# Moving a hybrid decoder layer's residual to DRAM for two thirds of its MLP, and computing four more quads by seven products

## The chip, the cores and the metric

The kernel runs on one core of a Trainium2 chip. The metric is the device time of one execution in microseconds; lower is better. An execution's own time is a little longer than its span, which runs from the first to the last instruction of the program.

## What is computed

One decoder layer on a sequence of 256 tokens, all in float32: an RMS norm, a combined input projection, eight attention heads and a pooling mixer, an output projection into the residual `x`, and then the part that this change is about, a gated MLP with a causal depthwise convolution between the up-projection and the gate:

```python
D_MODEL, SEQ, D_FF, CONV_WIDTH = 2048, 256, 5632, 3

def conv_ffn(h, w_up, conv_w, conv_b, w_down):
    u = h @ w_up
    u_pad = jnp.pad(u, ((0, 0), (CONV_WIDTH - 1, 0), (0, 0)))
    y = conv_b
    for i in range(CONV_WIDTH):
        y = y + conv_w[i] * u_pad[:, i:i + S]
    gate, val = jnp.split(y, 2, axis=-1)
    return (jax.nn.silu(gate) * val) @ w_down
...
    x = x + jnp.concatenate([a, m], axis=-1) @ w_out[l]
    x = x + conv_ffn(rms_norm(x, ffn_norm_g[l]), w_up[l], conv_w[l], conv_b[l], w_down[l])
```

## The kernel before

**Precision.** Every float32 matrix product is made of three float32r products: high by high, low by high and high by low, where `high` is the operand rounded to float32r and `low` what the rounding left. ACT makes the high part (`split_high`, L215), DVE the low part (`split_low`, L223 and L229).

**Chunks and steps.** All weights lie in DRAM as chunks of 128 x 2048 floats (1 MB). The program is a list of steps, two to a chunk. SP loads the chunks in order into four buffers, `raw`; the load of a chunk is issued when DVE has split the chunk that lay in its buffer (`release`, L290 and after). The high parts have a ring of four chunks, the low parts one of three, and splits are written five to six steps ahead of the products that use them. `hooks` (`after(u, f)`) hang further work on a step, in program order; each engine runs its own instructions in that order.

**The MLP** goes in thirds of 8, 8 and 6 hidden blocks of 256 features (`THIRDS`). The up stage of a third has 64 steps (48 in the last), each of 16 products into `ps_feat` (L313, L315); ACT and DVE evacuate, scale and add the convolution's taps, apply the gate, and split the result into `hid`. The down stage then multiplies `hid` by `w_down` in two passes of 1024 output columns (`down_pair`, `bp` 0 and 1). A pass goes quad by quad, a quad being one chunk: 2 blocks of hidden features by 2 halves of tokens by 2 halves of columns. An ordinary quad (`quad`, L982) takes 8 block products, 24 matmuls of 512 columns. A mixed quad (`quad_sums`, L919) takes 7 block products of sums and differences (Strassen's scheme in Winograd's form), 21 matmuls. The table `MIXED` names the mixed quads of each pass: 6 and 5 in a long third, 4 and 4 in the last, 30 in all.

**Sets.** A mixed quad needs sums of its weight blocks, in high and low parts: a set tile of 128 x 3072 (1.5 MB), of which there are four (`SETS`: 0 in the tag `s0`, 1 in the temporaries, 2 and 3 in the places `h2` and `h1` of `x2h`, the MLP's input, whose last blocks are therefore stored in DRAM as `tail` and loaded again before the next third). It also needs sums of its token halves, made by POOL (`token_sums`, L893) and kept in 20 cells, `sx`. Some sets are made in place in the down stage (`seven_sums`, DVE on `raw`). The other 16 (`STORED`: third, step, pass and quad they are for, steps ahead) are made during the up stage: SP loads the weights once more into `w` (1 MB, L251), ACT and DVE make the sums (L270 to L275, L243 to L247), POOL stores the differences `t` (512 KB, L262) and the set `s` (512 KB and 1 MB, L264). In the down stage SP loads the set back (1.5 MB, `load_set`, L267) and the quad's `raw` takes half of its data from `t`.

**Ends of a pass.** The residual sum `x2` (128 x 2 x 2048 floats, 2 MB) stays in SBUF. At the end of a pass the seven products' parts are added to it by DVE (`add_part`, L1035 to L1043); the ordinary products' banks are copied by ACT to a staging tile `st` in the place `s0` (`close`, L1089) and added to `x2` by two accumulating DMAs of 512 KB on POOL's queue (`add_by_dma`, L1012). Set 0 can be written again when these have landed. After the second pass of a long third (`behind`) the parts are copied to `st` first, and the additions follow in the next third's first steps.

## Time and profile before

| | |
|---|---|
| median of 3 runs | 1003.54 us (1003.36 to 1003.68) |
| the profiled execution | 1003.49 us, span 1001.6 us |
| PE busy | 997.1 us (100% of the span) |
| DVE busy | 858.9 us (86%) |
| ACT busy | 662.0 us (66%) |
| POOL busy | 144.3 us (14%) |
| DMA | 290.44 MB, 290 GB/s over the span |
| first long third, up stage and down stage | 179.7 and 79.6 us |
| second long third | 177.5 and 79.6 us |
| last third | 133.1 and 60.5 us |

A busy time is the time in which an engine had an instruction under way; the stages are read from the chain of waits, by the first matmul of each. The DMA share that the profile gives for a stretch is the mean busy share of the core's 16 DMA engines, which the queues of SP and POOL use together; it can come out slightly over 1. "To landing" is the time from a DMA's issue to the semaphore that tells its arrival.

### The profile page before, as it was taken

Reading aid. Unit: us, or ns where it says so; the run is one execution under the profiler, and the core shown is the slowest. Engines: PE = TensorE matmul, PEld = TensorE weight load, DVE = VectorE, ACT = ScalarE, POOL = GpSimd, SP = SyncE. Lnnn points to the kernel's source line nnn. Section 1 sums busy time; section 2 is a strip of 40 time slices with the busy share of each in tenths; the row PEclk is TensorE's granted clock in tenths of the full one; section 3 lists DMA queues with packets and bytes.
Section 4 is the critical chain, followed back from the end, with each engine's and each line's share of the span. In section 5 each row is a group of like instructions: output and inputs, shape, how many; then the busy total and the mean of one; then the engine's idle time right before and its main releaser. Section 6 shows DMA issues by size and latency. Waiting matters only on the chain.

```text
span 1001.6 us, 13775 instructions
## 1 busy us (share of the span) xinstructions
PE 997.1 (100%) x5205; PEld 856.7 (86%) x5205; DVE 858.9 (86%) x946; ACT 662.0 (66%) x1000; POOL 144.3 (14%) x178
## 2 busy tenths in 40 slices
PE   9999999999999999999999999999999999999998
PEld 8888888888888888888888888888888888888887
DVE  6989677898987989897987799998789869898898
ACT  6945575555566877787556577777766567777652
POOL 0220004700000122120000021321000002121110
PEclk9999999999999999999999999999999999999999
DMA  9775554474468899999898988989889897899894
GB/s 343 290 240 204 172 186 168 169 285 142 172 241 304 328 345 317 340 333 358 316 369 345 303 282 326 350 318 339 324 313 366 323 337 276 319 336 335 344 296 145
DMA packets 47170, 290.44 MB, mean 290 GB/s; under 512 B 5416, under 2 KB 6312, under 8 KB 19456
## 3 DMA queue, kind: packets, MB, share of 16 engines
q1 hardware_dynamic: 37456, 247.22, 67.4%
q0 software_dynamic: 9648, 42.34, 12.8%
q8 instruction: 41, 0.67, 0.3%
q14 instruction: 25, 0.20, 0.1%
HBM read 244.06 MB, written 39.19 MB: 283 GB/s over the span
## 4 chain that ended last, share of the span: by engine, by line
PE 99%; DVE 0%; issue 0%
PE ps_feat L313 35%; PE ps_feat L315 18%; PE ps_down L982 12%; PE ps_p L919 10%; PE ps_tok L300 9%; PE ps_down L919 7%; PE ps_v L307 4%; PE ps_pool L322 1%; PE ps_s L549 1%; PE ps_start L390 0%; PE ps_down L1004 0%; PE ps_T L536 0%; PE ps_x2T L766 0%; PE ps_av L582 0%; PE ps_eT L571 0%; PE ps_av L583 0%
## 5 line engine op out<-in xcount | busy, mean ns | idle before, releaser
L313 PE MATMUL ps_feat<-x2h,wh 128*128 128x512 f32 x1408 | 488.8, 392 | 0.0
L315 PE MATMUL ps_feat<-x2h,wl 128*128 128x256 f32 x1408 | 393.6, 280 | 0.0
L215 ACT ACTIVATE wh<-raw 128x1024 fp32r<-128x1024 f32 x358 | 360.1, 1048 | 16.2 <-DMA raw<-in_wts 12.9
L313 PEld LDWEIGHTS ps_feat<-x2h,wh 128*128 128x128 f32 x1408 | 264.2, 188 | 58.2
L229 DVE TENSOR_TENSOR wl<-raw,wh 128x2048 fp32r<-128x2048 f32 x116 | 266.8, 2307 | 31.1 <-ACT wh L215 16.8
L315 PEld LDWEIGHTS ps_feat<-x2h,wl 128*128 128x128 f32 x1408 | 264.3, 188 | 0.1
L223 DVE TENSOR_TENSOR wl<-raw,wh 128x1024 fp32r<-128x1024 f32 x126 | 156.9, 1268 | 10.4 <-ACT wh L215 6.6
L270 ACT ACTIVATE s<-raw 128x512 fp32r<-128x512 f32 (+1 forms) x38 | 32.0, 841 | 77.9 <-DVE raw L247 66.2
L835 ACT ACTIVATE y<-fs,pv 128x256 f32<-128x256 f32 x88 | 52.2, 593 | 45.0 <-DVE fs L822 45.0
L893 POOL TENSOR_TENSOR s<-y 128x128 f32<-128x128 f32 x34 | 34.5, 1014 | 291.4 <-DVE y L870 150.4
L270 ACT ACTIVATE s<-w 128x512 fp32r<-128x512 f32 (+1 forms) x32 | 26.8, 839 | 31.7 <-DMA w<-in_wts 31.7
L1012 POOL DMA_DIRECT2D x<-st x13 | 11.6, 930 | 241.9 <-ACT st L1089 195.0
L313 PE MATMUL ps_feat<-xh,wh 128*128 128x512 f32 x128 | 46.3, 402 | 0.0
L275 DVE TENSOR_TENSOR s<-w,s 128x512 fp32r<-128x512 f32 (+1 forms) x32 | 31.1, 973 | 15.5 <-ACT s L270 15.4
L601 ACT ACTIVATE fs<-ps_feat 128x512 f32<-128x512 f32 (+1 forms) x46 | 26.0, 565 | 25.3 <-PE ps_feat L315 25.3
L836 ACT ACTIVATE tap<-fs,pv 128x256 f32<-128x256 f32 x84 | 41.6, 495 | 0.0
L838 ACT ACTIVATE fs<-fs,pv 128x256 f32<-128x256 f32 x88 | 39.4, 495 | 0.0
L605 DVE TENSOR_TENSOR fs<-ps_feat,fs 128x512 f32<-128x512 f32 (+1 forms) x46 | 30.2, 659 | 8.4 <-ACT fs L601 8.4
L264 POOL DMA_DIRECT2D s<-s x32 | 17.3, 542 | 132.8 <-DVE s L275 132.5
L315 PE MATMUL ps_feat<-xh,wl 128*128 128x256 f32 x128 | 35.8, 280 | 0.0
L982 PE MATMUL ps_down<-wh,hid 128*128 128x512 f32 x144 | 35.6, 389 | 0.0
L300 PE MATMUL ps_tok<-wh,xh 128*128 128x512 f32 x128 | 35.5, 399 | 0.0
(268 smaller groups left out, 1589.1 us busy)
## 6 DMA issues: line engine op xcount, KB each, us to landing
raw<-in_wts SPq DMA_DIRECT2D x161, 1024.0 KB, 6.5
s<-s SPq DMA_DIRECT2D x16, 1536.0 KB, 8.7
w<-in_wts SPq DMA_DIRECT2D x16, 1024.0 KB, 8.1
s<-s POOLq DMA_DIRECT2D x16, 1024.0 KB, 10.6
raw<-in_wts SPq DMA_DIRECT2D x20, 512.0 KB, 5.8
t<-t POOLq DMA_DIRECT2D x16, 512.0 KB, 5.7
s<-s POOLq DMA_DIRECT2D x16, 512.0 KB, 6.7
raw<-t SPq DMA_DIRECT2D x16, 512.0 KB, 6.6
```

The source lines that it names most:

```text
L215: nc.scalar.activation(wparts[u][0], raw_of(u), AF.Copy)
L223: nc.vector.tensor_tensor(wpart(u, "wl"), raw_of(u), wparts[u][0].bitcast(F32), op=OP.subtract)
L229: nc.vector.tensor_tensor(whole(c, "wl"), raws[c], whole(c, "wh").bitcast(F32), op=OP.subtract)
L270: nc.scalar.activation(parts[0], w, AF.Copy)
L300: nc.tensor.matmul(ps[:, t, :], act[:, k0 + k, a, t * P:(t + 1) * P], w[:, k * 512:(k + 1) * 512], start=(first and k == 0 and n == 0), st ...
L307: nc.tensor.matmul(ps[:, t, :], act[:, k, a, t * P:(t + 1) * P], w[i], start=(first and n == 0), stop=(last and n == 2))
L313: nc.tensor.matmul(ps, wh[:, ws], act[:, k, :, :], start=(first and n == 0), stop=False, skip_group_check=True)
L315: nc.tensor.matmul(ps[:, S:], wl[:, ws], act[:, k, 0, :], start=False, stop=(last and n == len(ks) - 1), skip_group_check=True)
L835: nc.scalar.activation(y[:, m, :], u[:, m, :], AF.Identity, scale=cw[m][2], bias=col(C_CB + f0_ + m))
L836: nc.scalar.activation(a[:, m, :], u[:, m, :], AF.Copy, scale=cw[m][1])
L919: nc.tensor.matmul(ps, act[a], w[i], start=(first and n == 0), stop=(last and n == 2), skip_group_check=skip)
L982: nc.tensor.matmul(bank(t, b), hid(j, h, t)[a], part(w, b if h == 0 else 1 - b)[i], start=(n == 0 and h == 0 and (fresh or j == normal and ...
```

## The change

Four more quads become mixed: `MIXED` now has 7 quads in the first and 6 in the second pass of each long third, 34 in all, and eight sets of each long third are stored instead of six, 20 in all. To make room, `x2` leaves SBUF: it is written to DRAM (`parked`, 2 MB in two DMAs on POOL's queue) just before and at the first step of the MLP, and its place takes a fifth set tile (set 4) and four more cells for token sums (`more`). It is loaded back at step 43 of the last third. In between, each pass of the long thirds makes its whole sum in `st` (ACT's copy of the banks becomes two additions by DVE in the first pass) and adds it by accumulating DMA to `parked` in DRAM. All stored sets are made in set 4's tile; the weights for those of the long thirds are loaded by turns into two places (`cl` and `s0`, the column `odd`), every 6 steps instead of every 8 for most; the differences are made in place. Only one of the two tail blocks of `x2h` is stored and loaded in a long third, since set 3 is not used there. The loads of stored sets move from SP's queue to POOL's.

```diff
-MIXED = {8: ((0, 2, 3, 4, 5, 6), (0, 2, 3, 5, 6)), 6: ((0, 2, 3, 4), (0, 1, 2, 3))}
-SETS = {8: ({2: 2, 4: 3, 5: 1, 6: 2}, {0: 3, 2: 2, 3: 1, 5: 0, 6: 1}), 6: ({2: 3, 4: 2}, {0: 1, 1: 3, 2: 0, 3: 1})}
-STORED = ((0, 10, 0, 0, 0, 8), (0, 18, 0, 0, 2, 4), (0, 26, 0, 0, 4, 7), (0, 34, 0, 0, 6, 6), (0, 42, 0, 1, 0, 6), (0, 50, 0, 1, 2, 6), (1, 10, 1, 0, 0, 8), (1, 18, 1, 0, 2, 4), (1, 26, 1, 0, 4, 7), (1, 34, 1, 0, 6, 6), (1, 42, 1, 1, 0, 6), (1, 50, 1, 1, 2, 6), (2, 10, 2, 0, 0, 8), (2, 18, 2, 0, 2, 4), (2, 26, 2, 0, 4, 7), (2, 34, 2, 1, 1, 8))
+MIXED = {8: ((0, 1, 2, 3, 4, 5, 6), (0, 2, 3, 4, 5, 6)), 6: ((0, 2, 3, 4), (0, 1, 2, 3))}
+SETS = {8: ({0: 0, 1: 4, 2: 2, 3: 0, 4: 4, 5: 1, 6: 2}, {0: 4, 2: 1, 3: 2, 4: 4, 5: 0, 6: 1}), 6: ({2: 3, 4: 2}, {0: 1, 1: 3, 2: 0, 3: 1})}
+STORED = ((0, 8, 0, 0, 0, 7, 0), (0, 14, 0, 0, 1, 6, 1), (0, 20, 0, 0, 2, 4, 0), (0, 26, 0, 0, 4, 4, 1), (0, 32, 0, 0, 6, 6, 0), (0, 38, 0, 1, 0, 6, 1), (0, 44, 0, 1, 3, 8, 0), (0, 50, 0, 1, 5, 5, 1), (1, 2, 1, 0, 0, 7, 0), (1, 10, 1, 0, 1, 6, 0), (1, 18, 1, 0, 2, 4, 0), (1, 24, 1, 0, 4, 4, 1), (1, 30, 1, 0, 6, 6, 0), (1, 36, 1, 1, 0, 6, 1), (1, 42, 1, 1, 3, 8, 0), (1, 50, 1, 1, 5, 5, 1), (2, 10, 2, 0, 0, 8, 0), (2, 18, 2, 0, 2, 4, 0), (2, 26, 2, 0, 4, 7, 0), (2, 34, 2, 1, 1, 8, 0))
...
-    def early_load(c):
-        w = late["early"] = keep.tile([P, CH], F32, name="w", tag="cl")
+    def early_load(c, odd):
+        late["early", c] = w = (late["pool"] if odd else keep).tile([P, CH], F32, name="w", tag="s0" if odd else "cl")
         nc.sync.dma_start(w, wts[c])
...
     def load_set(c, i):
-        nc.sync.dma_start(late["tile"][i].bitcast(F32), stored[c][1])
+        nc.gpsimd.dma_start(late["tile"][i].bitcast(F32), stored[c][1])
...
+    def park(b):
+        if b == 0:
+            late["parked"] = dram.tile([P, NT, D], F32, name="parked")
+        c = slice(1024 * b, 1024 * b + 1024)
+        nc.gpsimd.dma_start(late["parked"][:, :, c], late["x2"][:, :, c])
+
+    def parked():
+        t = late["pool"].tile([P, 1024 * MORE // 4 + 3072], F32R, name="more", tag="x2")
+        late["more"] = t[:, :256 * MORE].rearrange("p (n a t) -> p n a t", a=2, t=P)
+        s = late["tile"][4] = t[:, 256 * MORE:]
+        late["s"][4] = set_parts(s)
+
+    def back():
+        late["x2"] = late["pool"].tile([P, NT, D], F32, name="x2", tag="x2")
+        nc.sync.dma_start(late["x2"], late["parked"])
...
+        def add_parked(t, src):
+            add_by_dma(late["parked"][:, t, 1024 * bp:1024 * (bp + 1)], src)
+
+        def parts():
+            pa_, p5, p7 = box["aux"], box["p5"], box["p7"]
+            nc.scalar.activation(block(0), pa_[:, 0, :], AF.Copy)
+            nc.vector.tensor_tensor(block(1), pa_[:, 1, :], block(0), op=OP.add)
+            nc.vector.tensor_tensor(block(2), p7, block(1), op=OP.add)
+            nc.vector.tensor_tensor(block(3), p5, block(2), op=OP.add)
+            nc.vector.tensor_tensor(block(1), p5, block(1), op=OP.add)
...
         def close(u):
...
+            if kind == "down" and not final:
+                if behind:
+                    for t in range(NT):
+                        nc.scalar.activation(box["st"][:, 1024 * (t + 1):1024 * (t + 2)],
+                                             box["tok"][t].rearrange("p b n -> p (b n)"), AF.Copy)
+                else:
+                    for t in range(NT):
+                        x = box["st"][:, 1024 * t:1024 * (t + 1)]
+                        nc.vector.tensor_tensor(x, box["tok"][t].rearrange("p b n -> p (b n)"), x, op=OP.add)
+                        add_parked(t, x)
+                    new_set()
+                return
...
+    after(f0 - 3, lambda: park(0))
+    after(f0, lambda: park(1))
+    after(f0 + 4, parked)
...
+    after(third[-1][0] + 43, back)
...
-        after(third[n][0] + at - 4, lambda c=(u0 + 8 * nq + b * 2 * nq + 2 * j) // 2: early_load(c))
+        after(third[n][0] + at - 3, lambda c=(u0 + 8 * nq + b * 2 * nq + 2 * j) // 2, odd=odd: early_load(c, odd))
+        if odd:
+            after(third[n][0] + at + 6, new_set)
```

**How it moves instructions.** Two places are shown. The first is SP's queue at the start of the first long third's up stage: `raw` are chunk loads, `w` the extra loads for stored sets, `tail` the blocks of `x2h`. Before:

```order
L176 DMA raw<-in_wts 128x2048 x19
L794 DMA tail<-x2h 128x3072 x2
L251 DMA w<-in_wts 128x2048
L176 DMA raw<-in_wts 128x2048 x4
L251 DMA w<-in_wts 128x2048
```

And with the change:

```order
L178 DMA raw<-in_wts 128x2048 x18
L253 DMA w<-in_wts 128x2048
L178 DMA raw<-in_wts 128x2048
L813 DMA tail<-x2h 128x3072
L178 DMA raw<-in_wts 128x2048 x2
L253 DMA w<-in_wts 128x2048
L178 DMA raw<-in_wts 128x2048 x3
L253 DMA w<-in_wts 128x2048
```

Half of the tail is left, the first `w` stands ahead of it, and a `w` follows every three chunk loads where it followed every four.

The second place is POOL's queue in the first long third's down stage: `s`, `more<-s` are sets, `x<-st` and `parked<-st` the accumulating DMAs of a pass's end, with the semaphores that each waits for. Before, the loads of sets were not in this queue:

```order
L264 DMA s_3742<-s_1786 128x2048 [waits DMASW2_49,DVE_49]
L1012 DMA x_1783<-st 128x1024 [waits DMASW3_49,DMAHW4_49,DVE_49,Activation_49]
L1012 DMA x_1783<-st 128x1024 [waits DMASW4_49,Activation_49]
L1012 DMA x_1783<-st 128x1024 [waits DMASW5_49,Activation_49]
L1012 DMA x_1783<-st 128x1024 [waits DMASW6_49,Activation_49]
```

And with the change:

```order
L268 DMA more<-s_2831 128x3072 [waits DMASW4_49,DMASW6_49,DMASW2_49,DMASW7_49,DMASW1_49,PE_49]
L268 DMA s_4087<-s_2993 128x3072 [waits DMAHW1_49,DMASW5_49,PE_49]
L268 DMA more<-s_3145 128x3072 [waits DMASW4_49,PE_49]
L268 DMA s_4087<-s_3301 128x3072 [waits DMASW5_49,PE_49]
L268 DMA more<-s_3456 128x3072 [waits DMASW6_49,PE_49]
L268 DMA s_4087<-s_3618 128x3072 [waits DMASW7_49,PE_49]
L1032 DMA parked<-st 128x1024 [waits DVE_49,Activation_49]
L1032 DMA parked<-st 128x1024 [waits DMASW3_49,DVE_49]
L268 DMA s_4339<-s_3770 128x3072 [waits DMASW3_49,DMASW2_49]
```

The last row is set 0 of the second pass's sixth quad (`j` 5): it is loaded behind the two accumulations of the first pass and waits until both have landed, since they read `st`, which lies in the same place.

## Rows read from the trace of the kernel before

**Rows 1.** Page, the chain that ended last, by engine.

```profile
PE 99%; DVE 0%; issue 0%
```

**Rows 2.** Windows by stage: PE, PEld, DVE, ACT, POOL busy, clock, DMA share, GB/s.

```profile
288.40:468.10 179.70, 179.70 (x1044) 158.43 (x1043) 157.36 (x163) 136.42 (x224) 30.94 (x42) 1.00 0.88 320
468.10:547.70 79.60, 79.60 (x353) 65.89 (x352) 67.69 (x57) 47.42 (x58) 1.80 (x2) 1.00 0.92 346
547.70:725.20 177.50, 177.50 (x1026) 156.29 (x1025) 155.58 (x148) 130.44 (x205) 33.67 (x44) 1.00 0.90 322
725.20:804.80 79.60, 79.60 (x353) 65.92 (x352) 67.67 (x57) 47.44 (x58) 1.81 (x2) 1.00 0.90 338
```

**Rows 3.** Chain in order of time: start us, us, engine, tile, line, count.

```profile
468.12 2.75 PE ps_p L919 x12
...
472.91 5.44 PE ps_down L982 x24
478.35 2.72 PE ps_p L919 x12
481.07 2.04 PE ps_down L919 x9
...
507.59 2.72 PE ps_p L919 x12
...
981.48 1.22 DVE wl L223
```

**Rows 4.** Groups by form, DVE's part of a stored set: busy us, mean ns, idle before.

```profile
L243 DVE TENSOR_TENSOR t<-w 128x1024 f32<-128x1024 f32 x16 | 22.7, 1418 | 0.0
L275 DVE TENSOR_TENSOR s<-w,s 128x1024 fp32r<-128x1024 f32 x16 | 19.5, 1219 | 0.0
L275 DVE TENSOR_TENSOR s<-w,s 128x512 fp32r<-128x512 f32 x16 | 11.6, 726 | 15.5 <-ACT s L270 15.4
L247 DVE TENSOR_TENSOR w<-w 128x512 f32<-128x512 f32 x16 | 11.1, 692 | 0.6
L246 DVE TENSOR_TENSOR w<-w,t 128x512 f32<-128x512 f32 x16 | 10.9, 684 | 0.0
```

**Rows 5.** Windows of 22 us, up stage, a stored set in each.

```profile
354.00:376.00 22.00, 22.00 (x129) 19.35 (x128) 18.96 (x19) 17.12 (x28) 3.70 (x8) 1.00 0.97 348
376.00:398.00 22.00, 22.00 (x129) 19.39 (x128) 21.62 (x23) 16.59 (x27) 6.33 (x6) 1.00 0.90 319
```

**Rows 6.** Waits: engine, line, waited for: us in total, times, longest.

```profile
ACT s L270 <- DMA w<-in_wts: 31.7, 14, 4.1
...
DVE wl L229 <- PE ps_feat L315: 7.8, 8, 1.3
```

**Rows 7.** Page, DMA issues: queue, count, KB each, median us to landing.

```profile
s<-s SPq DMA_DIRECT2D x16, 1536.0 KB, 8.7
...
s<-s POOLq DMA_DIRECT2D x16, 1024.0 KB, 10.6
```

**Rows 8.** Line L267, loads of sets: SP's wait for one, and time to landing.

```profile
L267 SPq EVENT_SEMAPHORE  x20: 17/28/4635, 452.7 to 957.0; - x20
...
DMA to landing us min/median/max: 6.4/8.7/14.8
```

**Rows 9.** Timeline of ACT at the end of a first pass: start us, us, [idle before].

```profile
507.18 1.94 ACT L1089 ACTIVATE st<-ps_down 128x1024 f32<-128x1024 f32 x2 [2.41 <-PE ps_down L982]
...
524.68 0.63 ACT L270 ACTIVATE s<-raw 128x512 fp32r<-128x512 f32 x1 [0.57 <-DMA x<-st]
```

**Rows 10.** Windows of 20 us in the down stage.

```profile
488.00:508.00 20.00, 20.00 (x90) 16.57 (x89) 17.41 (x15) 11.62 (x13) 0.00 (x0) 1.00 0.99 380
508.00:528.00 20.00, 20.00 (x90) 16.57 (x89) 17.06 (x14) 10.07 (x12) 1.80 (x2) 1.00 1.02 356
```

**Rows 11.** Groups: DVE's addition of 1024 columns from PSUM.

```profile
L1037 DVE TENSOR_TENSOR x<-ps_p,x 128x1024 f32<-128x1024 f32 x6 | 7.3, 1222 | 0.1
```

More of the change, by code (lines that the diff above doesn't have):

```diff
@@ L83, in cells @@
         for kind, n in wants:
-            tag = next(t for t, (a, b) in free.items() if a + n <= b)
+            tag = next(t for t in (free if kind == "hid" else ("sx", "x2", "cl", "c"))
+                       if free[t][0] + n <= free[t][1] and (t != "cl" or g >= 6))
             out[-1].append((kind, tag, free[tag][0], n))
@@ L1093, in close @@
                     nc.gpsimd.dma_start(out[:, t, 1024 * bp:1024 * (bp + 1)], x2[:, t, :])
-            elif not mixer and not behind:
-                new_set()
         end = final and bp == 1
@@ L1115, in down_pair @@
                     acts.append(save_parts)
-                for i, n in enumerate(() if behind else range(2) if heads else (4, 0, 1) if apart else (4, 0, 1, 2, 3) if mixer else range(5)):
+                if kind == "down" and not final and not behind:
+                    if at == s_end + 1:
+                        acts += [new_st, parts]
+                        run.adds = True
+                for i, n in enumerate(() if kind == "down" and not final else range(2) if heads else (4, 0, 1) if apart else (4, 0, 1, 2, 3) if mixer else range(5)):
                     if at == s_end + 1 + (i * (rest - 1) // 5 if end else 0):
```

120 lines of the change are left out of this document (68 added, 52 removed).

## The prediction

> **What bounds the kernel now.** I read the chain of waits first, then the windows by stage, then the waits and the DMA rows of the long thirds. The chain is PE for 99% of the span, with no idle time to speak of [rows 1], at a granted clock of 1.00 in every stage [rows 2]: only fewer matmuls make the kernel shorter, and anything else shows only where PE is made to wait. The chain in order of time prices a quad: an ordinary one is 5.44 us for 24 matmuls, a mixed one 2.72 + 2.04 = 4.76 us for 21 [rows 3], both 0.227 us a matmul. One other piece of the chain is not PE, DVE's 1.22 us at 981.48 in the last third [rows 3], which the change does not touch.
>
> The reader is to see how near the helpers are to PE. In the up stages DVE is busy 157.36 of 179.70 and 155.58 of 177.50 us, and the DMA engines have a share of 0.88 and 0.90; in the down stages the share is 0.92 and 0.90 [rows 2]. DVE is nonetheless ahead: 8 times a split waited for PE to free its buffer [rows 6]. ACT waited 31.7 us in all for the extra weights `w` [rows 6].
>
> **The change, part by part.**
>
> *Matmuls.* Four ordinary quads become mixed: the order of PE has 96 fewer matmuls at the ordinary line and 84 more at the mixed one, so the change does what it says. 12 x 0.227 = 4 x (5.44 - 4.76) = **2.72 us less**, all on the path.
>
> *Two more stored sets in each long third, spaced closer.* DVE's part of one set is 1.42 + 1.22 + 0.73 + 0.69 + 0.68 = 4.74 us [rows 4]. Two windows of 22 us hold 18.96 + 21.62 = 40.58 us of DVE with two sets in them [rows 5]; without the sets that is 31.1 us in 44 us. A step of the up stage lasts about 177.5/64 = 2.77 us, so the rest of DVE's work is 1.96 us a step. At a set every 8 steps DVE has 15.7 + 4.7 = 20.4 of 22.2 us; at one every 6 it has 11.8 + 4.7 = 16.5 of 16.6 us. That is full, but not over, and there are only seven such intervals in the first long third and four in the second, with looser steps behind them. Over the second up stage it is 155.6 + 2 x 4.7 = 165 of 177.5 us. I price it at nothing, covered by DVE's lead of up to three chunks, of which a set uses 4.7 us and the following steps give it back. If the cover goes, what is late next is the low part of a chunk, and PE waits.
>
> *The extra weights* are issued at the same place between chunk loads as before (the order of SP), but no longer wait for the one `w` buffer to be free. That can only shorten ACT's 31.7 us [rows 6]. I book no gain, since PE did not wait for it.
>
> *Bytes.* A stored set costs 1 MB of `w`, 0.5 MB of `t` and 1.5 MB of `s` in the up stage (3.15 million bytes), and 1.57 million to load in the down stage. The second up stage moved 322 GB/s x 177.5 us = 57.2 MB [rows 2]; with two more sets 63.5 MB, or 358 GB/s. The down stages moved 27.5 and 26.9 MB; with two more loads less one tail load each they move 29.1 and 28.5 MB in 78.2 us, 372 and 364 GB/s. The first up stage also gains the parking (2.1 MB) and saves a tail store (1.6 MB): 64.3 MB in 179.7 us, 358 GB/s. Can the engines do it? At full share the rows of before carry 322/0.90 = 358 and 320/0.88 = 364 GB/s with stores among the loads, and 346/0.92 = 376 without; single windows reach 380 [rows 2, 10]. So the demand is just within reach, and I price it at nothing, with a rival below. The Trainium skill, page "DMA: Bandwidth & Descriptors", section "Where 436 GB/s comes from", says that a core's HBM-to-SBUF transfers are bound at about 358 GB/s. The trace speaks against a ceiling there: 380 GB/s over 20 us [rows 10]. By the page the down stages of the change would last 81.3 and 79.6 us, 4.5 us more in all than by my sum, as an estimate from the page 1005.7.
>
> *Set loads on POOL's queue.* SP no longer stops for them; one such stop took 4.6 us [rows 8], with chunk loads queued behind it. In return a set load shares each engine with the chunk loads. No row shows such a load on POOL's queue. The nearest are the same loads on SP, 6.4 / 8.7 / 14.8 us to landing [rows 8], and POOL's 1 MB stores, 10.6 us [rows 7]. Three places have little room.
> - Set 2 for the third quad (`j` 2) can't start before the up stage's last matmul, since it lies in `h2`. It is used after two mixed quads and half of a 2.72 us piece: 2 x 4.76 + 1.36 = 10.9 us. Set 4 for `j` 4 has the same 10.9 us after `j` 1. With 8.7 us both fit; bounds 0 and 14.8 - 10.9 = 3.9 us each.
> - Set 0 for `j` 5 of the second pass is behind the two accumulations, which read `st` in its place. Before, the second pass began at 507.59 [rows 3], and ACT was let go by the landed accumulations at 524.68 [rows 9]: 17.1 us later. In the change the set is used after 4.76 + 5.44 + 3 x 4.76 + 1.36 = 25.8 us. That leaves 8.7 us for the load, just its median. Against it stands that DVE now makes the sums (2 x 1.22 us, [rows 11]) where ACT copied (1.94 us, [rows 9]), 0.5 us later. For it stands that one tail load and one set load fewer run in SP's queue beside the accumulations, where the share was 1.02 [rows 10]. Bounds 0 and about 6.5 us each; I take 0.2 us in each long third, near the median row: **0.4 us more**.
>
> *Parking and return.* The two stores of 1 MB fall at the start of the first long third and the load of 2 MB at step 43 of the last, both beside chunk loads; no one reads `x2` for long after. Nothing; up to 1 us each if chunks come late. Accumulating into DRAM instead of SBUF is not in the trace; it takes the same two DMAs of 512 KB, and if it were slower, it would show in set 0's bound.
>
> *Ends of the passes.* DVE's five additions (some 5 us) become four of 512 columns and two of 1024, 4 x 0.69 + 2 x 1.22 = 5.2 us [rows 4, 11]; ACT loses two copies. PE needs the banks only after 2.72 us of the next pass. Nothing.
>
> **Sum.** 1003.49 - 2.72 + 0.4 = 1001.2 us for the profiled execution, which lies 0.05 us below the median of 1003.54. I forecast **1001.2 us**, 0.23% less.
>
> **The rivals.**
> 1. *Set loads come late, and the gain is eaten.* If each of the two set-0 loads is 1.5 us late and the four others 0.3 us, the change costs 4.2 us of waits: 1003.49 - 2.72 + 4.2 = 1005.0; anywhere from 1001.6 to 1005.5 it is within 0.2% of before. For it: the room equals the median, and half of such loads were slower. Against it: the slow ones in before stood in SP's queue behind chunk loads and each other.
> 2. *The DMA engines become the bound in the up stages, and the kernel is slower.* The place is the seven intervals of 6 steps in the first long third: 3 chunks, one `w` and 2.1 MB of stores are 6.3 MB in 16.6 us, 378 GB/s, against 358 to 364 at full share [rows 2]. At 360 an interval would last 17.5 us, 0.9 us more; ACT waits for `w` and for the set's tile to be stored, DVE for ACT. Over seven and four intervals that is 10 us of lateness, against a lead of DVE of some 4 us in each long third once a set's own 4.7 us are taken; so 10 - 8 = 2 us at least, and 6 us where the lead is less. With rival 1's waits: 1001.2 + 2 + 3 = 1006, up to 1010. It decides for slower when the up stages together lose over 4.5 us. Against it: no `w` is loaded after step 47, so the rest of the stage can make up for it, and a window with 348 GB/s at 0.97 passed with PE busy throughout [rows 5]. A ceiling at the page's 358 would be this rival in the down stages; with 380 measured [rows 10] I give it 0.02 of the 0.20.
> 3. *No wait at all*, and DVE's piece of 1.22 us [rows 3] goes too, as the sums are no longer made in the temporaries: 1003.49 - 2.72 - 1.2 = 999.6.
>
> **How the numbers follow.** A measurement of this kernel can tell some 0.2%, 2.0 us, from no change. My forecast, with waits under 0.7 us in all, has a chance of 0.43 and counts as faster; rival 1 has 0.33 and counts as the same; rival 2 has 0.20 and counts as slower; rival 3 has 0.04, faster. So faster 0.47, same 0.33, slower 0.20. The range goes from 999.9, just above rival 3, to 1006.5, which leaves out the upper half of rival 2 and the set loads' upper bounds (2 x 6.5 us); the faster cases alone lie in 999.6 to 1001.5.
>
> **What would show it.** Right: the chain is PE alone in both long thirds, their down stages at 78.2 us each and up stages at 179.7 and 177.5. Rival 1: pieces of the chain that are DMA `s<-s` or `more<-s`, at the sixth quad of a second pass or the third or fifth of a first; the accumulations' time to landing, and that of the set loads on POOL's queue, tell which. Rival 2: up stages longer, DMA share at 1 from step 8 on, ACT's waits for `w` or for `more` longer than 31.7 us in all, and DVE's splits on the chain. My forecast is wrong in its size if the ordinary line loses other than 96 matmuls or a mixed quad is not 4.76 us, and wrong in its reason if PE's time is as forecast but idle time appears in the last third.

## The result: slower by 0.64%, lost in DVE's lead and at the passes' ends

The changed kernel takes 1010.56 us in the median of 5 runs (1007.05 to 1011.19), the one before 1003.54 us (1003.07 to 1003.93): a ratio of 1.0064, with a 95% interval of 1.0046 to 1.0082. The forecast was 1001.2 us. The change also scatters over 4 us where the kernel before, run beside it, scatters over 0.9 (2.2 to 3.9 in the 9 to 23 runs of it beside the experiments). The profiled execution took 1009.67 us, with a span of 1007.6 us.

The chain of waits by engine, which was PE for 99% before [rows 1]:

```profile
PE 62%; DVE 20%; DMA 10%; issue 5%; ACT 3%; POOL 0%; DVEq 0%; SPq 0%; ACTq 0%; POOLq 0%
```

The long thirds' stages in the windows view, as in [rows 2] (stretch, its length, PE, PEld, DVE, ACT and POOL busy with their instructions, granted clock, DMA share, GB/s):

```profile
289.06:468.84 179.78, 179.78 (x1045) 158.51 (x1044) 167.77 (x175) 140.06 (x229) 45.37 (x55) 1.00 0.93 353
468.84:550.27 81.43, 79.43 (x347) 64.38 (x346) 67.59 (x59) 44.93 (x56) 5.09 (x8) 1.00 0.95 357
550.27:728.39 178.12, 177.77 (x1025) 156.28 (x1024) 162.10 (x157) 131.93 (x207) 43.37 (x56) 1.00 0.93 350
728.39:810.09 81.70, 79.39 (x347) 64.45 (x346) 69.40 (x61) 46.72 (x60) 5.08 (x8) 1.00 0.95 363
```

The clock is 1.00 throughout, so the loss is waiting. By the sum the down stages should last 79.59 - 1.36 = 78.23 us; they last 81.43 and 81.70 us, 6.7 us over plan together. The up stages are 0 and 0.6 us over. DVE's time in the up stages grew from 157.4 and 155.6 to 167.8 and 162.1 us. Inside the first one it hardly rests:

```profile
332.00:354.00 22.00, 22.00 (x129) 19.35 (x128) 21.62 (x22) 16.07 (x27) 7.11 (x8) 1.00 0.90 336
...
376.00:398.00 22.00, 22.00 (x128) 19.36 (x128) 21.58 (x23) 17.21 (x27) 5.08 (x6) 1.00 1.01 388
398.00:420.00 22.00, 22.00 (x129) 19.38 (x128) 21.62 (x22) 16.69 (x28) 6.00 (x7) 1.00 0.97 370
420.00:442.00 22.00, 22.00 (x129) 19.39 (x128) 21.58 (x23) 18.03 (x28) 6.89 (x10) 1.00 0.95 366
```

Before, such full windows took turns with looser ones (18.96 and 21.62 [rows 5]), 118.5 us of work in the 132 us from 310 to 442; now three full ones follow one another, and the same stretch holds 125.9. PE still runs without a gap here: it lives on splits made ahead. What that costs is seen in the chain in order of time (start, length, what), from the end of the up stage (468.84) to the start of the second pass:

```profile
451.88 2.20 DVE wl L231
454.08 0.61 DVE fs L606
454.79 0.55 issue
455.33 2.30 DVE wl L231
457.64 14.41 DMA raw<-in_wts
472.08 1.06 ACT wh L217
...
482.60 1.23 DVE wl L225
483.87 0.98 PE ps_p L939 x3
...
493.34 1.23 DVE s L287
494.59 10.07 DMA raw<-in_wts
504.76 2.01 ACT wh L217 x2
507.29 0.70 DVE st L1097
508.01 0.70 DVE st L1098
...
512.14 1.23 DVE st L1135
513.41 2.34 PE ps_down L939 x9
```

Read it from the top: DVE piece after piece without rest, then a chunk load that could leave only when DVE had freed its buffer and that took 14.4 us, then again DVE, a chunk of 10.1 us, ACT's split of it, the four additions of the parts (L1097 and after), and at last the close (L1135), whose banks PE wants. The end of the pass in the time order of the engines, first ACT, then DVE, then PE (start, length, form; in brackets the idle time before and what ended it):

```profile
504.76 2.01 ACT L217 ACTIVATE wh<-raw 128x1024 fp32r<-128x1024 f32 x2 [5.77 <-DMA raw<-in_wts]
506.67 0.58 ACT L1096 ACTIVATE st<-ps_p 128x512 f32<-128x512 f32 x1
...
507.29 0.69 DVE L1097 TENSOR_TENSOR st<-ps_p,st 128x512 f32<-128x512 f32 x1 [5.36 <-ACT st L1096]
...
509.94 2.28 DVE L231 TENSOR_TENSOR wl<-raw,wh 128x2048 fp32r<-128x2048 f32 x1
512.14 2.35 DVE L1135 TENSOR_TENSOR st<-ps_down,st 128x1024 f32<-128x1024 f32 x2
...
508.85 0.70 PE L939 MATMUL ps_p<-wh,sx 128*128 128x512 f32 x2 [0.64 <-DVE st L1098]
...
513.41 0.73 PE L939 MATMUL ps_down<-wh,sx 128*128 128x512 f32 x2 [1.00 <-DVE st L1135]
```

ACT's copy of a finished part stands in its queue behind the split of a chunk that is not there; DVE's additions wait for that copy; a low part of 2.28 us stands between them and the close. In the kernel before ACT copied the banks at 507.18 [rows 9], with nothing of DVE in between. By the starts of the matmuls PE lost 0.82 + 0.49 + 1.18 us at this place, and the last piece again, 1.19 us, in the next third. What PE's weight loads waited for in all (engine, line, releaser: us, times, longest), where before almost nothing stood:

```profile
PEld ps_down L939 <- DVE st L1135: 2.8, 2, 1.4
PEld ps_p L939 <- DMA s<-s: 1.4, 1, 1.4
PEld ps_p L939 <- DVE st L1100: 1.1, 2, 0.7
PEld ps_p L939 <- DVE wl L225: 1.1, 2, 0.6
...
PEld ps_p L939 <- DMA more<-s: 0.8, 1, 0.8
```

The two waits for sets lie in the second long third, as does one of 0.6 us in its up stage. And the DMA issues that answer to [rows 7, 8] (KB each, median us to landing):

```profile
s<-s POOLq DMA_DIRECT2D x14, 1536.0 KB, 10.4
...
more<-s POOLq DMA_DIRECT2D x6, 1536.0 KB, 9.6
parked<-st POOLq DMA_DIRECT2D x8, 512.0 KB, 9.4
```

### The profile page after: what moved, and what is told of

The parts are those of the page before. It is cut to its first block, busy times and chain, and to the rows that moved or that the text cites. A ratio compares the mean times of both kernels' runs of the same rounds, so it can differ in the third digit from the quotient of the medians.

```text
span 1007.6 us, 13870 instructions
## 1 busy us (share of the span) xinstructions
PE 997.4 (99%) x5193; PEld 853.8 (85%) x5193; DVE 876.6 (87%) x970; ACT 663.6 (66%) x1004; POOL 177.3 (18%) x220
## 4 chain that ended last, share of the span: by engine, by line
PE 62%; DVE 20%; DMA 10%; issue 5%; ACT 3%; POOL 0%; DVEq 0%; SPq 0%; ACTq 0%; POOLq 0%
PE ps_feat L314 17%; PE ps_tok L301 9%; PE ps_down L1002 9%; PE ps_feat L316 9%; DVE wl L231 8%; PE ps_p L939 7%; PE ps_down L939 6%; DMA w<-in_wts 4%; DMA raw<-in_wts 3%; PE ps_v L308 3%; DVE more L276 2%; ACT wh L217 2%; DVE y L863 2%; DMA s<-s 1%; DVE fs L606 1%
## 5 line engine op out<-in xcount | busy, mean ns | idle before, releaser
L217 ACT ACTIVATE wh<-raw 128x1024 fp32r<-128x1024 f32 x358 | 360.0, 1048 | 20.8 <-DMA raw<-in_wts 20.7
L225 DVE TENSOR_TENSOR wl<-raw,wh 128x1024 fp32r<-128x1024 f32 x126 | 157.0, 1269 | 7.9 <-ACT wh L217 5.5
L271 ACT ACTIVATE s<-raw 128x512 fp32r<-128x512 f32 (+1 forms) x34 | 28.6, 840 | 82.5 <-DVE raw L249 82.4
L913 POOL TENSOR_TENSOR s<-y 128x128 f32<-128x128 f32 x38 | 40.7, 1071 | 115.0 <-DVE y L890 115.0
L271 ACT ACTIVATE more<-w 128x512 fp32r<-128x512 f32 (+1 forms) x40 | 33.6, 840 | 37.7 <-DMA w<-in_wts 32.6
L276 DVE TENSOR_TENSOR more<-w,more 128x512 fp32r<-128x512 f32 (+1 forms) x40 | 38.7, 968 | 12.9 <-ACT more L271 12.9
L265 POOL DMA_DIRECT2D s<-more x40 | 22.3, 557 | 118.2 <-DVE more L276 115.0
L939 PE MATMUL ps_p<-wh,sx 128*128 128x512 f32 x120 | 37.4, 392 | 0.9 <-DVE st L1098 0.6
L308 PE MATMUL ps_v<-wh,xh 128*128 128x512 f32 x128 | 35.2, 398 | 0.0
L301 PE MATMUL ps_tok<-wh,cat 128*128 128x512 f32 x128 | 34.4, 390 | 0.0
```

Source lines behind the costliest of these rows:

```text
L217: nc.scalar.activation(wparts[u][0], raw_of(u), AF.Copy)
L225: nc.vector.tensor_tensor(wpart(u, "wl"), raw_of(u), wparts[u][0].bitcast(F32), op=OP.subtract)
L271: nc.scalar.activation(parts[0], w, AF.Copy)
L276: nc.vector.tensor_tensor(parts[1], w, parts[0].bitcast(F32), op=OP.subtract)
L301: nc.tensor.matmul(ps[:, t, :], act[:, k0 + k, a, t * P:(t + 1) * P], w[:, k * 512:(k + 1) * 512], start=(first and k == 0 and n == 0), st ...
L308: nc.tensor.matmul(ps[:, t, :], act[:, k, a, t * P:(t + 1) * P], w[i], start=(first and n == 0), stop=(last and n == 2))
```

## The experiments

Times are medians, with the ratio to the kernel before, run on the same chip, and its 95% interval. Line numbers are those of the changed kernel, and all edits are to it. The stages, from first matmul to first matmul (us), are those of the one profiled execution of each kernel, which need not be the median of its runs (1011.44 us in e0, 1011.26 in e5, 1012.96 in e10, 1011.37 in e14):

```
                               up 1   down 1   up 2   down 2   median
plan, 34 mixed quads           179.8   78.2    177.5   78.2
plan, 32 mixed quads           179.8   78.9    177.5   78.9
before                         179.8   79.6    177.5   79.6    1003.54
the change                     179.8   81.4    178.1   81.7    1010.56
e0  the change again           180.6   83.7    178.1   81.5    1009.82
e1  set loads on SP            180.2   85.1    177.5   85.1    1014.63
e2  close first                181.2   81.5    179.3   81.5    1009.07
e3  seven sets (32 quads)      179.8   80.0    177.5   79.8    1004.49
e4  e3 and close first         179.8   79.2    177.5   79.5    1003.62
e5  one less in pass 2 (32)    180.8   83.1    177.5   81.9    1008.92
e6  e3 and an idle load        179.8   79.8    177.5   79.9    1003.76
e7  made in place, close first 179.8   82.5    177.5   86.3    1012.97
e8  early load                 179.8   81.1    179.4   81.9    1010.96
e9  early load, close first    179.8   83.5    180.3   80.8    1012.38
e10 no accumulations           180.2   84.2    179.6   81.6    1009.16
e11 split first                180.9   82.4    177.5   80.9    1008.99
e12 light sets                 179.8   80.7    177.5   80.6    1005.90
e13 e12 and close first        179.8   79.6    177.5   80.2    1005.21
e14 close and split first      182.2   81.1    179.6   81.2    1008.36
e15 e12, close, split first    179.8   78.8    177.5   80.9    1004.12
e16 seven sets, 34 quads       179.8   83.6    177.5   83.4    1013.76
```

**e0, the change again.**

> The changed kernel once more, unaltered, to see how far its own runs differ and where. From the first trace (1009.67 us): both long down stages 81.4 and 81.7 us against a planned 78.2, up stages 179.8 and 178.1 against 179.7 and 177.5. Theory (chunks come late in the first pass of a down stage, where set loads and chunk loads keep the DMA engines full): 1007 to 1011 us, the down stages again 3 us or more over plan, the up stages within 1 us. Rival (the up stages are short of DMA or DVE time in most runs): a slower run shows up stages longer by 2 us or more.

1009.82 us (1007.16 to 1011.44), ratio 1.0050 (1.0033 to 1.0068). The down stages are 5.5 and 3.3 us over plan, the up stages 0.8 and 0.6. The time is as the theory had it; the waits are of the same kinds, but now the loads of the second and third quad's sets cost 0.98 and 0.80 us in the first third too.

**e1, set loads back on SP's queue.**

```
-        nc.gpsimd.dma_start(late["tile"][i].bitcast(F32), stored[c][1])
+        nc.sync.dma_start(late["tile"][i].bitcast(F32), stored[c][1])
```

> All set loads go back from POOL's queue to SP's, at the same steps. If the turns that the two queues take are what makes chunks late (theory), the chunk before the close lands some 3 to 4 us earlier, ACT no longer waits 5 us for it, and the down stages lose 2 to 3 us each less: 1004 to 1006 us. If the engines are just full (rival), the bytes are the same, and the time stays at 1008 to 1011 us. If SP's stops for a free set are worse than the turns (second rival): over 1011 us, with waits of SP at the set loads of 4 us and more.

1014.63 us, ratio 1.0101 (1.0077 to 1.0125): the second rival. PE now waits for sets, in front of all else:

```profile
PEld ps_p L939 <- DMA more<-s: 8.1, 4, 3.1
PEld ps_p L939 <- DMA s<-s: 6.6, 4, 1.8
```

The second rival had SP stop for 4 us and more at the set loads; the longest such wait was 2.7 us. What grew is the loads' time to landing, 11.7 us in the median against 9.9 on POOL's queue. POOL's queue was the right choice; sharing the engines by turns is not what costs.

**e2, the close ahead of the low part.**

```
+        wait_low = has(u, "adds") and has(u + 1, "first")
-        if ahead - 1 < n and not placed:
+        if ahead - 1 < n and not placed and not wait_low:
             split_low(ahead - 1)
...
+        if has(u, "first"):
+            split_low(ahead - 2)
```

> In the first pass of both long down stages the low part of the one chunk that stands between DVE's four additions and the close (2.3 us) is made after the close. Theory (the banks come free late because DVE reaches the close late): the two gaps of 1.18 and 1.19 us at the start of the second pass go, and little else changes: 2.0 to 2.5 us less than the changed kernel of the same job. Rival (the chunk itself is the shortage, its low part then comes 2.4 us late): the gaps turn up some us later as waits for wl, no gain.

1009.07 us, 0.75 us under e0 where 2.0 to 2.5 were expected, with intervals that overlap. The waits on the close are gone from the trace, as the theory said; the sets' (0.4 to 1.0 us each), those on the parts (0.3 to 0.5 us) and three on the splits of the up stages (0.66, 0.40 and 1.30 us) are there instead. Part of the cause, not the main one.

**e3, seven sets.**

```
-MIXED = {8: ((0, 1, 2, 3, 4, 5, 6), (0, 2, 3, 4, 5, 6)), ...
+MIXED = {8: ((0, 2, 3, 4, 5, 6), (0, 2, 3, 4, 5, 6)), ...
-STORED = (..., (0, 14, 0, 0, 1, 6, 1), ..., (1, 10, 1, 0, 1, 6, 0), ...
```

> The second quad of the first pass is an ordinary one again in both long thirds, so seven stored sets in each, one set load of 1.57 MB and one extra set in the up stage less; two quads of 0.68 us are given back, 1.36 us more of PE work. Theory (the DMA engines are full in the first pass): the late chunk, the late set of the third quad and the late close go in both, 3 us and more gained for 1.36 paid: 1003 to 1006 us, the down stages 78.9 to 79.5 us. Rival (the close or the adding in DRAM is what costs): the gaps at the second pass stay, 1010 to 1012 us.

1004.49 us, ratio 1.0007 (0.9998 to 1.0017): 5.3 us under e0 although 1.36 us are paid, the up stages at plan, and of all waits only the close's left (1.00 and 0.77 us). The time is the theory's, but the edit takes away three things at once: a load, the set's making in the up stage, and a mixed quad. e5 to e7 part them.

**e4, seven sets and the close first.** The edits of e2 and e3.

> Seven stored sets and the close ahead of the low part, both in both long thirds. The profile of seven sets alone had two waits left, 1.00 and 0.77 us, both on the close. Theory (full DMA engines cost the late loads, DVE's order the late close, and the two add up): both waits go, 1.7 us less than seven sets alone: 1002.4 to 1003.0 us, at or just under the kernel before. Rival (the low part is then late in their place): 1004 us or more, with waits for wl some us into the second pass.

1003.62 us, ratio 0.9996 (0.9988 to 1.0005): no wait over 0.2 us is left, 1.1 us better than e3 against the kernel before, with intervals that overlap; the theory's 1002.4 to 1003.0 us was not reached. This is the best complete version found; it can't be told from the kernel before.

**e5, one set and quad less in the second pass instead.**

```
-... (0, 2, 3, 4, 5, 6)), 6: ...
+... (0, 2, 3, 5, 6)), 6: ...
-STORED = (..., (0, 44, 0, 1, 3, 8, 0), ..., (1, 42, 1, 1, 3, 8, 0), ...
```

> The same saving as with seven sets (one stored set and one mixed quad less in each long third, the same matmuls), but taken from the second pass: its fifth quad is ordinary, and the set of its fourth quad is made in place again; the first pass keeps its seven mixed quads. Theory (the shortage is in the first pass, whose seven set loads and chunk loads keep the engines full): the first pass's late set loads, late chunk and late close stay, and 1.36 us of work is paid: 1009 to 1011 us. Rival (any 1.57 MB less in a third relieve it, or the up stage's spacing was what cost): 1004 to 1005 us as with seven sets.

1008.92 us, ratio 1.0043 (1.0028 to 1.0058). The time is just under the theory's, the waits are so only in part: those at the second pass's start stay (0.84 + 0.49 + 1.19, then 0.49 + 1.18 us), and 0.8 us for `wl` come in each second pass, whose fourth set is made in place again; but of those for sets in the first pass only 0.3 us is left, though its loads are unchanged. So the end of the first pass suffers from its seventh mixed quad, and the waits for sets from something that one early set less in the up stage cures.

**e6, seven sets and an idle load.**

```
+        if (b, j) == (0, 4) and nq == 8:
+            after(u - 12, lambda c=c: load_set(c, 4))
```

> Seven sets, with the removed load put back alone: at the place of the second quad's set load, POOL's queue loads the fifth quad's set into the same memory once more, 1.57 MB that nobody uses; no matmul and no work of ACT or DVE is added, and the fifth quad's own load comes as before. Theory (bytes on full engines in the first pass): late set of the third quad and late chunks come back, down stages 1.5 to 2.5 us longer each than with seven sets: 1007 to 1009 us. Rival (the second quad's own need is what cost, not the bytes): 1004 to 1005 us.

1003.76 us, ratio 0.9996 (0.9987 to 1.0005). My theory fell here: 1.57 MB more in each first pass cost nothing. The DMA share of its first 20 us is 0.99 as in the change, and no wait for a set comes. Full engines alone are not the cause.

**e7, the second quad's set made in place.** The two `STORED` entries of e3 go, `MIXED` stays; with e2's edit.

> All 34 mixed quads, with the second quad's set in the first pass made in place from its own chunk and not stored: no load of 1.57 MB, and DVE has about 4.9 us more to do near the end of the long up stages. Close ahead of the low part as well. Theory (with the bytes gone DVE's lead carries this): down stages at 78.3 to 78.8 us, 1001.2 to 1002.5 us, under the kernel before. Rival (DVE is full at the up stage's end): waits for wl of 2 us and more at the passage from up to down stage, 1003 to 1007 us.

1012.97 us, ratio 1.0086 (1.0072 to 1.0099): the rival's reason, at 6 us above its range. The load is saved, the quad is there, and 4.9 us of DVE's work come at the end of the up stage; PE waits 1.75 and 3.59 us in the first quad of the down stages, for banks of the up stage that DVE has not read yet, and 1.86 us for `wl`. DVE is what is short.

**e8, the second quad's set loaded earlier, and e9, the same with the close first.**

```
-(0, 14, 0, 0, 1, 6, 1) ... (1, 10, 1, 0, 1, 6, 0)
+(0, 14, 0, 0, 1, 9, 1) ... (1, 10, 1, 0, 1, 9, 0)
```

> The set load of the first pass's second quad is issued three steps before its place in the change, so that it stands ahead of POOL's last token sums of the up stage (4 us of work that begin only when DVE has made the values) instead of behind them; all else as in the change. In the profile of the change this load left at 463.95 us, 4.9 us before the down stage began; with seven sets and an idle load, at 8.1 us before, and the same bytes cost nothing there. Theory (what costs is when these bytes come: 4 us late, they hold up the chunk that the second pass's start hangs on): the load leaves 8 us before the stage, that chunk lands in 8 us instead of 10, and the waits of 1.0 us for the second and third quad's set go: 1006.0 to 1007.5 us. Rival (the seventh mixed quad in the pass leaves too little time whatever the loads do): 1009 to 1011 us.

> The early load of the second quad's set and the close ahead of the low part, with all 34 quads and eight stored sets. Theory: the waits for sets, about 1 us each, and the close's 1.2 us go in both thirds, and what is left are the waits of the up stages and small ones on wl: 1003.5 to 1006 us. Rival (the waits only move on to wl): 1007 to 1010 us.

1010.96 us, ratio 1.0063 (1.0046 to 1.0080), and 1012.38 us, ratio 1.0078 (1.0052 to 1.0103): the rivals, e9 2.4 us above its rival's range. In e8 the load left 8.6 us before the stage and the waits for sets shrank to 0.8 us, but another came for it, on the low part of the fourth quad, whose chunk the load had delayed (2.04 us in e8, 3.18 in e9). The waits of e8:

```profile
PEld ps_p L939 <- DVE wl L225: 3.1, 3, 2.3
PEld ps_down L939 <- DVE st L1135: 2.7, 2, 1.4
...
PEld ps_p L939 <- DMA s<-s: 0.8, 2, 0.4
```

With so little lead in hand, serving one transfer earlier made the next one late.

**e10, no accumulations.** The call in `add_parked` (L1032) goes.

> The eight accumulations into DRAM are left out, so the residual lacks the sums of the first two thirds; all else as in the change. Theory (they come after the chunk that the second pass's start hangs on, and their set load was in time): nothing gained in the down stages' first pass, under 1 us in all, 1008.5 to 1010.5 us. Rival (the accumulations into DRAM hold up loads): 3 us and more less, 1007 us or under.

1009.16 us, ratio 1.0055 (1.0029 to 1.0081): nothing gained within the scatter. The waits in both first passes are of e0's kinds, and one of 1.1 us for `wl` besides.

**e11, the fourth quad's low parts ahead of the last value.** In the second quad's first step the splits are written ahead of the step's own work:

```
+                run.behind = kind == "down" and not final and (bp, j, h) == (0, 1, 0)
...
+        sums = sums and not has(u, "behind")
```

> In the first pass's second quad, DVE makes the low parts of the fourth quad's chunk and set before the last value's taps and product (2.06 us) instead of after them, as it did when that quad was an ordinary one; nothing else moves. Theory (the buffer for the pass's last chunk is freed 2 us late, that chunk and those behind it come late, and the second pass's start hangs on one of them): that chunk is issued some 14 us after the stage's start instead of 16.1, and the waits at the second pass's start shrink from 2.5 us to about 1; 1.5 us less in each long third, 1006 to 1008.5 us. Rival (the order of these rows is hidden): 1009 to 1011 us, 16 us and 2.5 us as before.

1008.99 us, ratio 1.0047 (1.0030 to 1.0065): 0.8 us under e0's median, inside the change's scatter and just above the theory's 1006 to 1008.5. The mechanism shows in the trace. A mixed quad's step is written ahead of the splits, an ordinary one's behind them; so the change put the up stage's last value (L863, L890) ahead of L225 and L287, which free the buffer of the pass's last chunk. In e11 they are back in front:

```profile
481.94 0.69 DVE L249 TENSOR_TENSOR raw<-raw 128x512 f32<-128x512 f32 x1
482.55 1.22 DVE L225 TENSOR_TENSOR wl<-raw,wh 128x1024 fp32r<-128x1024 f32 x1
483.82 1.23 DVE L287 TENSOR_TENSOR s<-raw,s 128x1024 fp32r<-128x1024 f32 x1
484.96 0.68 DVE L863 TENSOR_TENSOR y<-y,tap 128x510 f32<-128x510 f32 x1
```

That chunk is issued 20.8 us ahead of its use instead of 17.6 to 18.3, and the waits at the second pass's start are 0.3 and 0.7 us. The set waits (1.04, 0.99 and 1.32 us) stay, and two of 0.5 and 0.7 us for the low parts come in the first third.

**e12, light sets.**

```
-        after(at + 2, lambda c=c: last_sums(late["early", c], late["early", c]))
+        if n == 2:
+            after(at + 2, lambda c=c: last_sums(late["early", c], late["early", c]))
```

> The two last subtractions of each of the sixteen early sets of the long thirds (1.4 us of DVE for each set) are left out, so the products of these sets are wrong; every load and store stays. Theory (DVE is full in the up stages and comes into the down stages without its lead): the up stages are at 179.8 and 177.5 us, chunks are issued 27 us ahead of their use at the stage's start instead of 23 to 26, the waits for sets and for wl in the first pass go, and only the close's stay: 1005 to 1006.5 us. Rival (the DMA engines are the bound, and the bytes are the same): 1009 to 1011 us.

1005.90 us, ratio 1.0024 (1.0014 to 1.0033): the theory. DVE's busy time in the up stages is back near that of before (158.7 and 154.8 us against 157.4 and 155.6), with the loads and stores of the change. The up stages are at plan, every wait for a set is gone, and what stays are the waits at the second pass's start (2.2 and 2.1 us). The windows of its first third, up stage and the first 20 us of down stage, and those 20 us in the change:

```profile
287.88:467.66 179.78, 179.78 (x1045) 158.45 (x1044) 158.68 (x159) 140.36 (x229) 46.93 (x55) 1.00 0.94 362
...
468.00:488.00 20.00, 20.00 (x90) 16.55 (x89) 17.65 (x18) 12.91 (x19) 1.64 (x3) 1.00 0.87 330
```

```profile
468.00:488.00 20.00, 19.93 (x89) 16.16 (x88) 16.64 (x18) 14.21 (x21) 1.64 (x3) 1.00 0.99 400
```

At the same bytes the up stage moved 362 GB/s where the change moved 353, and the down stage began with the engines at 0.87 instead of 0.99. That is 1.6 MB more in the up stage and 1.4 MB less in the first 20 us behind it: in the change the engines were full there with loads that DVE had held up.

**e13, light sets and the close first.**

> The same with the close ahead of the low part; again products of the sixteen sets are wrong. Theory (DVE's lost lead and its late close are the whole loss): both long down stages at 78.2 to 78.8 us, the time of my forecast, 1001 to 1003 us, at the same bytes as the change. Rival (the engines hold up chunks whatever DVE does): 1005 us or more, the down stages at 80 us and more.

1005.21 us, ratio 1.0020 (1.0010 to 1.0030), the down stages at 79.6 and 80.2 us. The time is the rival's, if barely, and the down stages lie between the two: one wait of 0.4 us in the first third, on the parts; in the second the parts are late (0.51 + 0.49 us), after a last chunk that landed 7.1 us ahead of its use.

**e14, close first and split first, nothing left out.**

> Both order edits together, the close ahead of the low part and the fourth quad's low parts ahead of the last value, with nothing left out. Theory: the second pass starts without a wait; the waits for sets and the up stages' stay: 1005.5 to 1008 us. Rival (the waits only move on, as with the early load): 1009 to 1012 us.

1008.36 us, ratio 1.0049 (1.0032 to 1.0067), between the two and no better than e0's 1.0050. The second pass starts without a wait in both thirds; those for sets (0.51 to 1.31 us each) and in the up stages (0.67, 1.43 and 1.67 us) are there in full. Without the lead, the order edits alone gain nothing that can be measured.

**e15, light sets with both order edits.**

> Sixteen early sets without their two last subtractions (their products are wrong), the close ahead of the low part, and the fourth quad's low parts ahead of the last value; all loads and stores of the change stay. Theory (DVE's lost lead, the late close and the late buffer are the whole loss): the last chunk of the first pass lands 11 us or more ahead of its use instead of 7 to 8, no wait over 0.3 us in either third, both long down stages at 78.3 to 79.3 us: a span of 1000.0 to 1001.5 us, a median of 1001.5 to 1004. Rival (the engines hold up chunks by themselves): waits of 0.5 us and more stay in one of the first passes, down stages at 79.6 us or more as in the run before.

1004.12 us, ratio 1.0003 (0.9994 to 1.0012). The last chunk lands 13.7 and 14.6 us ahead. In the first third the down stage is at 78.82 us, 0.6 over plan; in the second it is at 80.89:

```profile
467.06:545.88 78.82, 78.52 (x347) 64.71 (x346) 67.46 (x58) 44.62 (x55) 5.09 (x8) 1.00 0.92 346
...
723.38:804.27 80.89, 79.89 (x347) 64.27 (x346) 67.47 (x58) 44.62 (x55) 5.07 (x8) 1.00 0.92 338
```

The median is just above the theory's 1004. The first third is the theory's but for a wait of 0.49 us on `wl`; the second's down stage is the rival's, 79.6 us or more. So the three causes are most of the loss, not all: there the chunk for the second pass's second quad took 9.8 us to land, and the parts waited for ACT again (0.60 + 0.49 us), besides 0.49 us on `wl`. What holds that chunk up is open.

**e16, seven sets and 34 quads.** `STORED` has seven entries in each long third, 7 or 8 steps apart, the second pass's fourth quad is made in place; with both order edits.

> All 34 quads with seven stored sets in each long third, 7 or 8 steps apart, the fourth quad's set of the second pass made in place, and both order edits; nothing left out. Theory: the up stages are at plan as with seven sets, the first pass has no wait, and the in-place set costs a wait for wl of 0.8 us in each second pass, as it did when it was last made there: 1002 to 1003.5 us, under the kernel before. Rival (DVE, in the second pass full to nine tenths, cannot take 4.9 us more): 1004 to 1007 us.

1013.76 us, ratio 1.0109 (1.0092 to 1.0126): the rival's reason, at nearly 7 us above its range. Up stages at plan, and but for waits of 0.47 and 0.3 us nothing in the first passes; nearly all is lost in the second passes, where the waits of 2.06, 0.49, 1.98 and 2.07 us are for DVE's low parts:

```profile
PEld ps_p L939 <- DVE wl L225: 9.5, 9, 2.3
```

One more thing adds to e7, e9 and e16: after PE's wait of 3.6, 3.2 and 2.1 us, the granted clock was at 0.50, the lower of its two levels, for 3.4 us, and eight matmuls that followed started 0.43 us apart instead of 0.23, some 1.7 us in each run. In all other runs, e1 with a wait of 2.9 us among them, it stayed at 1.00 until PE was done.

How far ahead of its use on PE a chunk's load was issued shows DVE's lead, since DVE frees the buffers (us, first and second long third, read from the traces):

```
                     first quad of pass 1: issued    last quad of pass 1: issued, landed
before                    27.5, 28.4                     20.9, 20.9      15.8, 16.0
the change                25.7, 23.5                     17.6, 18.3       7.7,  8.0
e0  again                 23.7, 23.5                     17.6, 18.2       8.0,  8.4
e3  seven sets            27.5, 27.6                     20.9, 20.9      16.1, 15.8
e11 split first           23.7, 24.1                     20.8, 20.8       9.4, 12.4
e12 light sets            29.1, 28.5                     18.3, 18.3       6.9,  6.9
e15 all three             29.7, 29.1                     20.8, 20.8      13.7, 14.6
```

Two causes stand apart here: the first column follows DVE's load in the up stage, the second the order of the rows in the second quad. The first column also tells where PE waits for sets. Read in the same way from the change, e0, e2, e5 and e10 to e16, whose early sets are loaded from POOL's queue at the change's places, it is 23.5 to 24.1 us in eleven long thirds, and in each PE waits 1.2 to 2.1 us in all for the second and third quad's sets; it is 25.5 us or more in the other eleven, and there these waits are 0.5 us at most.

## Why the prediction was wrong

**Right: the matmuls.** The ordinary line lost 96 and the mixed gained 84, and without waits the time is there: e15's first down stage is within 0.6 us of the planned 78.23.

**Wrong, the main step: "I price it at nothing, covered by DVE's lead of up to three chunks, of which a set uses 4.7 us and the following steps give it back."** The rate was right: 16.5 of 16.6 us was forecast, 21.6 of 22 measured. But at that rate the steps give nothing back, and the looser steps behind the tight ones were too few: the last set is at step 50 of 64, and in the first long third DVE was still busy for 20.0 of the 21 us from 447 to 468 (17.5 before). DVE entered the down stages 2 to 5 us behind where it was before, with chunks issued 23.5 to 25.7 us ahead instead of 27.5 to 28.4. The bill came a stage later than the work that ran it up: waits for the sets of the second and third quad, for low parts, and scatter from run to run. Taking 1.4 us off each set brought the median from 1009.82 to 1005.90 us and the ratio to the kernel before from 1.0050 to 1.0024, so 2.6 to 3.9 us; that is the largest term.

**Wrong: "PE needs the banks only after 2.72 us of the next pass. Nothing."** I counted the additions' length, not what stands ahead of them in the queues: ACT's split of a late chunk, and a 2.3 us low part between the additions and the close. It cost 2.5 us in the change's first long third and 3.1 in e0's; the close alone 1.2.

**Missed: an order row that I did not look at.** A quad that becomes mixed turns the order of its step and the splits round. Two microseconds of DVE's work came ahead of the release of one buffer, and the chunk behind it was issued 3 us later. e11 takes it back. No term of the sum stood for it. Its share of the time is not settled beyond e13 to e15, 1005.21 to 1004.12 us, with intervals that overlap.

**Set loads.** "With 8.7 us both fit; bounds 0 and 14.8 - 10.9 = 3.9 us each": the loads took 9.9 us in the median and up to 13.6, and the waits where they came were 0.4 to 1.3 us, inside the bounds. The third quad's load took 12.1 to 12.3 us where it was late (the change's second third, e0), 10.3 in the change's first third and 8.0 in e12's. The second quad's set was not among my three places: its load stands in POOL's queue behind the up stage's last token sums, which wait for DVE's last values (L890), and so left 4.9 us ahead of the down stage in the change's first third and 3.0 us ahead in its second and in both of e0, where it was late. So these waits were a consequence: with DVE relieved (e12) that load left 8.0 us ahead, and the same loads from the same queue were never waited for. The 0.4 us for set 0 behind the accumulations did not show; that set was in time, and e10 gains nothing.

**The rivals.** The time is near rival 2's 1010, and so is its order of events (DVE's lead gone, sets tight); the ceiling that it builds on, DMA engines that carry no more than some 360 GB/s, is not there. With DVE lighter the up stages carried 362 and 363 GB/s without a wait, and the first 20 us of the down stage in the change 400. The Trainium skill's bound of about 358 GB/s, page "DMA: Bandwidth & Descriptors", section "Where 436 GB/s comes from", does not hold in these stretches; 400 GB/s is measured. One link of rival 2's chain is there: in the second up stage DVE waited 8.0 us for ACT's part of the sets (4.6 before), and ACT 13.2 us for `w` (12.0 before). e12 has the same wait of DVE (8.4 us) and none of PE in that stage; what it costs at the change's load no run shows. Rival 3's piece stayed: PE's weight load at that place in the last third waited 0.6 us before and in the change. I gave the right sign 0.20 because I asked whether DVE would be over its limit, not what it would still have in hand at the stage's end.

**Open.** Why e15's second down stage is 2.7 us over plan. That is most of the last 2.9 us between e15's 1004.12 us and the forecast: in the profiled execution the rest is 0.6 us in the first down stage and 0.5 in the last, less 0.9 us ahead of the MLP, where the kernels' executions differ by up to 1.8 us. How the loss divides between the second and third cause is open too, since without the first they gain nothing that can be measured (e14).

## What to carry to other kernels

An engine that is busy for 98% of a long stretch and still in time can win back no lead that it loses there: book the lead as a stock, with what goes in and out of it, and ask what it is when the next stage begins, which needs it more. Where a stage looks short of DMA, see first who issues the loads; a load that waits for a buffer makes the engines idle now and full later, and moving or reordering transfers then only moves the wait (e1, e8, e9), while taking work off the engine that frees the buffers ends it (e12). And when a step changes its kind, print the order around it on every engine: the rows that turned round here put a load 3 us later, and no term of the sum held it.

## What the runs showed of the hardware

- The same 1.5 MB set loads took 6.4 to 14.8 us from SP's queue before [rows 8]; on POOL's queue, beside chunk loads, 7.2 to 13.6 us, median 9.9. Putting them back on SP (e1), in line with the chunk loads, cost 4.8 us against e0; they took 8.1 to 13.7 us, median 11.7.
- The 512 KB accumulations into DRAM landed in 9.4 us in the median, beside chunk loads, and held up nothing that showed (e10).
- The DMA engines carried 400 GB/s over 20 us at a share of 0.99 (the change, loads of chunks and sets), and 362 GB/s over a whole up stage with stores among them (e12).
- After a wait of PE of 3.6, 3.2 and 2.1 us the granted clock was at 0.50 for 3.4 us (e7, e9, e16); after one of 2.9 us in e1 it stayed at 1.00.
